# The recurrence's gate products and scans are written behind the first keys, queries and values of the forgetting attention

## The chip, the core and the metric

The kernel runs on one core of a Trainium2 chip. Its time is device time in microseconds (us), from one execution of the whole program. TensorE is written PE, VectorE DVE, ScalarE ACT, GpSimd POOL and SyncE SP. Each of them runs its own instructions strictly in the order in which they stand in its queue.

## The reference, cut to what matters

Two layers (DEPTH = 2) of a sequence encoder, 512 positions of 1024 channels, float32. Each layer mixes the positions by three branches, A, B and C, merges them with sigmoid gates, and is followed by a SwiGLU block and a gated embedding:

```
h = rmsnorm(x); z = h @ w_in            # one projection, cut into u, u_gelu, c_q, c_kv, fq, fk, fv, f_logit, gates
A: xc = causal conv of width 4 over u;  r, i = sigmoid(xc @ wa + ba), sigmoid(xc @ wx + bx)
   a = exp(-8 r softplus(-lam));  h_t = a_t h_(t-1) + sqrt(1 - a_t^2) i_t xc_t;  y_a = (h * gelu(u_gelu)) @ w_br_a
C: 8 heads: softmax(fq fk / 8 + cum_t - cum_s, causal) fv, cum = cumsum(logsigmoid(f_logit));  y_c = ... @ w_br_c
B: 8 heads of latent attention with rotary keys;  y_b = ... @ w_br_b
merged = sum over A, B, C of sigmoid(gate) * y;  x = x + merged @ w_o;  then SwiGLU and the embedding
```

The diff concerns A (the two gate products `wa`, `wx`, and the scan) and the start of C (keys and queries of heads 0 and 1, and the values of all heads).

## The kernel before

Activations lie transposed, channels on 128 partitions and the 512 positions along the row. Every float32 product is made of three matmuls of a high and a low part (`mm3`: high x high, high x low, low x high), each 128 x 128 by 512 columns. A projection of 1024 channels onto 128 (`dense`) is thus 24 matmuls into one PSUM bank, and the values of all heads (`values`) are 96 matmuls into four banks.

The weights come as one stream, in the order in which the code asks for them: SP loads units of 128 x 512 into four buffers (`raw`), and each unit is split into its two parts, the high one by a copy on ACT (L112), the low one by a subtraction on DVE (L113), into five buffers (`hl`). A unit feeds 12 matmuls, and a buffer is split anew only after PE has used it up.

Activations in split form lie in pages `pr`, plain ones in 20 pages `pf`. A page or a bank that is taken waits for its last reader. The file gives the order in which the work is written; from it a scheduler makes each engine's fixed queue when the program is built, and it may move an instruction ahead of others that would wait. It lets the splits of the weights go first.

Inside `mix(layer)`, which makes the three branches, the order is: the projections `u` with the convolution (`ev_u`: the split pages `xcp[t]` feed the gate products), the key and forget column (`key_and_forget`, whose logarithm runs on POOL), four projections for the GeLU (`ev_ug`), and then the part that the diff moves:

- the gate loop: for each of four tiles t two products of three matmuls with `xcp[t]`, and `lru_gate(t)`: on ACT two tanh out of PSUM, one exp and one tanh of the page, on DVE one instruction;
- `lru_tail`: four square roots on ACT (another function table), and for each t on DVE a fused multiply, a multiply, the scan, a fused multiply with the GeLU page, and a split into `yA[t]` (a copy on ACT, a subtraction on DVE). It then frees the pages.

After them come `fox_proj(0)` (keys `k0` and queries `q0`, 24 matmuls each, and `ev_heads`, which places them in pages for two heads and lets POOL fetch the forgetting rows), `values`, and the attention of branch C. `attention` goes through 32 blocks of 128 queries (8 heads by 4): scores S on PE, mask, maximum, exponential, normalisation on DVE and ACT, transposes on PE (L830), a split of the transposed block into `pth` (ACT, L855) and `ptl` (DVE), and, when four blocks of a head are there, the product with the values (`pv_mm`, here PV). Between the blocks it fills in matmuls of other work from a `plan`: for the first eight blocks the next heads' keys (here k1), the gates and products of branch A for two column blocks (`mg(0, 0, yA)` and `mg(0, 1, yA)`, which need all four `yA`), the reload and renormalising of x (`renorm`: eight loads on POOL, eight fused multiplies and eight subtractions on DVE, eight copies on ACT), and the next heads' queries (q1).

In the attention `self.V`, `yA` and the pages of heads 0 and 1 are what the moved part has to have made.

Of the kernel before, what the change touches and what calls it, by code (L numbers as in the profile page):

```python
# [166 lines left out]
class Trunk:  # L167
# [273 lines left out]
    def mix(self, layer):  # L441
        nc = self.nc
        L, st, X = layer, self.st, self.xp
# [6 lines left out]
        xcp = [None] * 4  # L450
# [91 lines left out]
        later = [pf.take(), pf.take()]  # L542
# [59 lines left out]
        def fox_proj(p, X, r):  # L602
            return [
                self.dense(self.win(L, C_FK + 128 * p), X, ev_heads(kp, p, r, True, False)),
                self.dense(self.win(L, C_FQ + 128 * p), X, ev_heads(qp, p, r, True, True)),
            ]

        def values(spec, X, rT):

            V = []  # L610
            bs = [self.banks.take() for _ in range(NT)]
            for k, x in enumerate(X):
                wh, wl = self.w.wide(spec + (k,))
                for j in range(NT):
                    c = slice(j * 128, (j + 1) * 128)
                    self.mm3(bs[j][:, :], x.h[:, c], x.l[:, c], wh, wl, k == 0, k == len(X) - 1)
                    yield
            for j in range(NT):
                g = pr.take()
                V.append(g)  # L620
                dst = g.ap.rearrange("p (h t d) -> p h t d", h=HEADS, t=2)
                src = bs[j].rearrange("p (h d) -> p h d", h=HEADS)
                hi = dst[:, :, 0, :]
                if rT is None:
                    self.split(hi, dst[:, :, 1, :], src)
                else:
                    r = rT[:, j:j + 1]
                    self.act(hi, src, AF.Copy, scale=r)
                    self.stt(dst[:, :, 1, :], src, r, hi.bitcast(F32), ALU.mult, ALU.subtract)
                self.banks.give(bs[j])  # L630
            self.V = V
# [6 lines left out]
        def lru_gate(t):  # L638
            def f(bR, bI):
                r, i = pf.take(), pf.take()  # L640
                self.act(r.ap, bR[:, :], AF.Tanh, bias=self.v(L, V_BA + t), scale=0.5)
                self.act(i.ap, bI[:, :], AF.Tanh, bias=self.v(L, V_BX + t), scale=0.5)
                self.banks.give(bR), self.banks.give(bI)
                s = self.sp[:, 4 * L + t:4 * L + t + 1]
                e = self.msp[:, 4 * L + t:4 * L + t + 1]
                a = pf.take()
                self.act(a.ap, r.ap, AF.Exp, bias=e, scale=e)
                last_tanh.append(self.act(r.ap, r.ap, AF.Tanh, bias=s, scale=s))
                self.stt(i.ap, i.ap, 1.0, xc[t].ap, ALU.add, ALU.mult)
                xc[t].free()  # L650
                xcp[t].free()
                aT[t], bT[t], tT[t] = a, i, r
            return f

        for t in range(4):
            bb = []
            for g in range(2):
                b = self.banks.take()
                wh, wl = self.w.tile(("lru", L, g, t))
                self.mm3(b[:, :], wh, wl, xcp[t].h, xcp[t].l, True, True)  # L660
                bb.append(b)
            lru_gate(t)(*bb)
        for p in later:
            p.free()

        def lru_tail():

            with ExitStack() as after:
                for i in last_tanh:
                    after.enter_context(self.tc.issue_after(i.ins))  # L670
                for q in tT:
                    self.act(q.ap, q.ap, AF.Sqrt, bias=self.eps[:, 1:2])
            for t in range(4):
                a, bb, q = aT[t], bT[t], tT[t]
                self.stt(q.ap, a.ap, 1.0, q.ap, ALU.add, ALU.mult)
                self.tt(bb.ap, bb.ap, q.ap)
                nc.vector.tensor_tensor_scan(q.ap, a.ap, bb.ap, 0.0, op0=ALU.mult, op1=ALU.add)  # L677
                self.stt(q.ap, q.ap, 0.25, gx[t].ap, ALU.mult, ALU.mult)
                yA[t] = pr.take()
                self.split(yA[t].h, yA[t].l, q.ap)  # L680
                for p in (q, a, bb, gx[t]):
                    p.free()

        lru_tail()
        k0, q0 = fox_proj(0, X, st["r"])
        self.run(k0)
        self.run(q0)
        self.run(values(("fv", L), X, rT))
        Xn = [None] * KD

        def renorm(*ks):
# [317 lines left out]
        for j in range(KD):  # L1009
            p = pf.take()  # L1010
# [381 lines left out]
```

## Time and profile before

| | before |
|---|---|
| median of 3 runs | 1827.87 us (1827.26 to 1827.97) |
| the profiled execution | 1827.03 us |
| its span, first to last instruction | 1825.3 us |
| mean granted TensorE clock | 0.995 |
| PE busy | 1804.1 us (99%) |
| DVE busy | 1210.6 us (66%) |
| ACT busy | 817.7 us (45%) |
| POOL busy | 117.0 us (6%) |

Busy time is the sum over the span; in a stage an engine with a low sum can still be full. In a timeline row the columns are the start, the length of the merged run (the last instruction's end, which overlaps the next start), engine, line, operation, output and inputs, count, and in brackets the idle time before it with what ended it. In a row of windows each engine has its busy time in the stretch and its count, then come the granted clock of PE, the DMA share and GB/s.

### The profile page before, as it was taken

What the parts mean: (1) busy time and instruction counts of PE and PEld (TensorE: products, weight loads), DVE (VectorE), ACT (ScalarE), POOL (GpSimd) and SP (SyncE); (2) the same over time, 40 slices, a digit from 0 to 9 for tenths busy, and PEclk for the clock granted to TensorE, in tenths of its full rate; (3) what the DMA queues carried; (4) which work ended last, traced back from release to release, by engine and by line L of the source; (5) the groups of instructions that cost most, each with busy time, mean ns of one, the idle gap of its engine ahead of it and who ended that gap; (6) DMA issues with size and microseconds to landing.
All of it is one profiled execution on the core that took longest, in us unless ns stands there. A gap on an engine that the chain in (4) does not pass through costs nothing. (4 is left out here: it accounts for less than half of the span.)

```text
span 1825.3 us, 24128 instructions
## 1 busy us (share of the span) xinstructions
PE 1804.1 (99%) x8476; PEld 1502.0 (82%) x8476; DVE 1210.6 (66%) x2421; ACT 817.7 (45%) x1562; POOL 117.0 (6%) x234
## 2 busy tenths in 40 slices
PE   9899999999999999999999999999999999999998
PEld 7678888888888888888887788888888888888887
DVE  7897678866665555444778966888576655553457
ACT  4765556553333333223447655565533333332243
POOL 1230001100000000000103200010000000000000
PEclk9899999999999999999999999999999999999999
DMA  5152223324222232322433322242242322233331
GB/s 189 59 151 82 78 80 116 96 73 139 94 98 94 97 98 98 109 94 98 132 111 122 105 81 82 89 118 85 86 129 92 99 98 96 95 110 99 98 116 47
DMA packets 98827, 184.17 MB, mean 101 GB/s; under 512 B 13553, under 2 KB 14753, under 8 KB 98705
## 3 DMA queue, kind: packets, MB, share of 16 engines
q1 hardware_dynamic: 89280, 162.04, 27.0%
q0 software_dynamic: 8416, 19.45, 3.9%
q8 instruction: 66, 1.08, 0.2%
q10 hardware_dynamic: 1008, 1.14, 0.2%
q14 instruction: 57, 0.46, 0.1%
HBM read 173.98 MB, written 4.21 MB: 98 GB/s over the span
## 5 line engine op out<-in xcount | busy, mean ns | idle before, releaser
L237 PE MATMUL bank<-pr,hl 128*128 128x512 f32 (+1 forms) x6812 | 1600.8, 392 | 7.6 <-ACT pr L233 6.9
L237 PEld LDWEIGHTS bank<-pr,hl 128*128 128x128 f32 (+1 forms) x6812 | 1268.5, 188 | 271.0 <-ACT pr L233 8.6
L112 ACT CAST hl<-raw 128x512 fp32r<-128x512 f32 x590 | 364.2, 618 | 670.3 <-PE bank L237 394.5
L113 DVE TENSOR_TENSOR hl<-raw,hl 128x512 fp32r<-128x512 f32 x590 | 404.3, 685 | 379.8 <-ACT hl L112 361.7
L221 DVE TENSOR_TENSOR pf<-pf 128x512 f32<-128x512 f32 (+3 forms) x235 | 151.1, 651 | 31.8 <-ACT pf L230 29.8
L221 DVE TENSOR_TENSOR pf<-bank,pf 128x512 f32<-128x512 f32 (+3 forms) x198 | 132.9, 676 | 57.3 <-PE bank L237 32.6
L230 ACT ACTIVATE pf<-pf 128x512 f32<-128x512 f32 (+1 forms) x145 | 86.1, 600 | 113.2 <-DVE pf L221 110.5
L237 PE MATMUL bank<-pr 128*128 128x256 f32 (+5 forms) x704 | 120.3, 302 | 3.3 <-ACT pf L230 2.5
L237 PEld LDWEIGHTS bank<-pr 128*128 128x128 f32 (+1 forms) x704 | 102.6, 190 | 13.7 <-ACT pf L230 3.3
L221 DVE TENSOR_TENSOR pr<-pf,pr 128x512 fp32r<-128x512 f32 (+3 forms) x126 | 85.5, 682 | 4.5 <-ACT pr L233 3.1
L230 ACT ACTIVATE pf<-bank,small 128x512 f32<-128x512 f32 (+3 forms) x130 | 68.9, 531 | 37.7 <-DVE small L838 34.8
L233 ACT CAST pr<-pf 128x512 fp32r<-128x512 f32 (+2 forms) x114 | 70.3, 620 | 29.5 <-DVE pf L218 20.3
L855 ACT CAST pth<-bank 128x128 fp32r<-128x128 f32 (+3 forms) x128 | 54.1, 427 | 58.5 <-PE bank L830 52.0
L221 DVE TENSOR_TENSOR ptl<-bank,pth 128x128 fp32r<-128x128 f32 (+3 forms) x128 | 61.7, 485 | 13.8 <-ACT pth L855 9.1
L838 DVE TENSOR_REDUCE small<-bank 128x1 f32<-128x128 f32 (+3 forms) x128 | 61.7, 483 | 7.6 <-PE bank L237 6.5
L237 PE MATMUL bank<-hl,pr 128*128 128x512 f32 x240 | 56.2, 390 | 0.3 <-DVE hl L113 0.3
L830 PE MATMUL bank<-identr,pf 128*128 128x128 f32 x320 | 55.0, 273 | 0.0
L237 PEld LDWEIGHTS bank<-hl,pr 128*128 128x128 f32 x240 | 44.8, 188 | 10.0 <-DVE hl L113 0.7
L225 DVE TENSOR_SCALAR pf<-pf,small 128x128 f32<-128x128 f32 (+3 forms) x128 | 48.6, 383 | 2.7
L230 ACT ACTIVATE pf<-bank,vec 128x512 f32<-128x512 f32 x60 | 41.0, 688 | 14.2 <-PE bank L237 13.8
L830 PEld LDWEIGHTS bank<-identr,pf 128*128 128x128 f32 x320 | 40.1, 140 | 8.2
L218 DVE SCALAR_TENSOR_TENSOR pf<-pf,bank 128x512 f32<-128x512 f32 x48 | 32.6, 683 | 20.8 <-PE bank L237 20.4
(112 smaller groups left out, 793.9 us busy)
## 6 DMA issues: line engine op xcount, KB each, us to landing
raw<-wst SPq DMA_DIRECT2D x606, 256.0 KB, 2.6
pf<-xT POOLq DMA_DIRECT2D x16, 256.0 KB, 3.4
pr<-pr POOLq DMA_DIRECT2D x32, 128.0 KB, 2.6
pf<-xs POOLq DMA_DIRECT2D x16, 256.0 KB, 3.3
pf<-trig POOLq DMA_DIRECT2D x12, 256.0 KB, 3.2
pf<-xT SPq DMA_DIRECT2D x8, 256.0 KB, 5.4
xs<-pf POOLq DMA_DIRECT2D x8, 256.0 KB, 2.7
pf<-pT POOLq DMA_DIRECT2D x4, 256.0 KB, 3.0
```

The costliest lines, as they stand in the source:

```text
L112: self.nc.scalar.copy(hi, src)
L113: self.nc.vector.tensor_tensor(lo, src, hi.bitcast(F32), op=ALU.subtract)
L218: self.nc.vector.scalar_tensor_tensor(out, a, s, b, op0=op0, op1=op1)
L221: self.nc.vector.tensor_tensor(out, a, b, op=op)
L225: self.nc.vector.tensor_scalar(out, a, s1, None, op0=op0)
L230: return self.nc.scalar.activation(out, a, f, **kw)
L233: self.nc.scalar.copy(hi, src)
L237: self.nc.tensor.matmul(out, a, b, start=start, stop=stop, skip_group_check=True)
L830: nc.tensor.transpose(T[:, c], p2.ap[:, c], self.ident[:, :])
L838: nc.vector.reduce_max(R[t][:, 0:1], S[:, :m], axis=AX.X, negate=True)
L855: self.nc.scalar.copy(hi, src)
```

## The change

The gate loop, with the freeing of two pages behind it, and the call of `lru_tail` move behind `k0`, `q0` and `values`. Nothing else is edited; the same instructions are issued, and the weight stream is packed in the new order.

```diff
@@ in mix(), after key_and_forget and the four GeLU projections
-        for t in range(4):
-            bb = []
-            for g in range(2):
-                b = self.banks.take()
-                wh, wl = self.w.tile(("lru", L, g, t))
-                self.mm3(b[:, :], wh, wl, xcp[t].h, xcp[t].l, True, True)
-                bb.append(b)
-            lru_gate(t)(*bb)
-        for p in later:
-            p.free()
-
         def lru_tail():
...
-        lru_tail()
         k0, q0 = fox_proj(0, X, st["r"])
         self.run(k0)
         self.run(q0)
         self.run(values(("fv", L), X, rT))
+        for t in range(4):
+            bb = []
+            for g in range(2):
+                b = self.banks.take()
+                wh, wl = self.w.tile(("lru", L, g, t))
+                self.mm3(b[:, :], wh, wl, xcp[t].h, xcp[t].l, True, True)
+                bb.append(b)
+            lru_gate(t)(*bb)
+        for p in later:
+            p.free()
+
+        lru_tail()
```

How the queues change, from the built programs. First PE in layer 0, from the last GeLU projection (bank1) on. Before (`hl` are split weights, `pr` split activations; where `hl` stands first the product is one of `values`):

```order
L237 MATMUL bank1_68<-pr_65,hl_64 128x512 x24
L237 MATMUL bank2_69<-pr_65,hl_64 128x512
L237 MATMUL bank3_70<-pr_65,hl_64 128x512
L237 MATMUL bank4_71<-pr_65,hl_64 128x512
L237 MATMUL bank7_74<-pr_65,hl_64 128x512
L237 MATMUL bank0_67<-pr_65,hl_64 128x512
L237 MATMUL bank5_72<-pr_65,hl_64 128x512
L237 MATMUL bank6_73<-pr_65,hl_64 128x512
```

The same place now:

```order
L237 MATMUL bank1_68<-pr_65,hl_64 128x512 x24
L237 MATMUL bank2_69<-pr_65,hl_64 128x512 x24
L237 MATMUL bank3_70<-pr_65,hl_64 128x512 x2
L237 MATMUL bank4_71<-hl_64,pr_65 128x512
L237 MATMUL bank7_74<-hl_64,pr_65 128x512
L237 MATMUL bank3_70<-pr_65,hl_64 128x512 x22
```

The gate products, one matmul to each of eight banks, are gone from here, and k0 (24 matmuls into bank2) and q0 (bank3) follow the GeLU projections at once.

The second place is PE in layer 0 where the first transposes of the attention stand (L830), before:

```order
L237 MATMUL bank3_70<-pr_65,hl_64 128x512 x14
L237 MATMUL bank0_67<-pr_65 128x256 x2
L237 MATMUL bank3_70<-pr_65,hl_64 128x512 x8
L237 MATMUL bank5_72<-pr_65,hl_64 128x512 x18
L830 MATMUL bank7_74<-identr_77,pf_66 128x128
L237 MATMUL bank5_72<-pr_65,hl_64 128x512 x5
L830 MATMUL bank2_69<-identr_77,pf_66 128x128 x2
L237 MATMUL bank5_72<-pr_65,hl_64 128x512
L830 MATMUL bank4_71<-identr_77,pf_66 128x128 x3
L830 MATMUL bank6_73<-identr_77,pf_66 128x128 x4
```

Now (bank5 x24 is the gate of `mg(0, 1)`; bank0 and bank7 are the products of branch A with `yA`):

```order
L237 MATMUL bank5_72<-pr_65,hl_64 128x512 x24
L237 MATMUL bank1_68<-pr_65 128x128 x2
L237 MATMUL bank6_73<-pr_65 128x512 x2
L830 MATMUL bank7_74<-identr_77,pf_66 128x128
L237 MATMUL bank0_67<-pr_65,hl_64 128x512
L830 MATMUL bank2_69<-identr_77,pf_66 128x128 x2
L830 MATMUL bank4_71<-identr_77,pf_66 128x128 x3
L237 MATMUL bank0_67<-pr_65,hl_64 128x512 x3
L237 MATMUL bank7_74<-pr_65,hl_64 128x512 x4
L237 MATMUL bank0_67<-pr_65,hl_64 128x512 x3
```

Fewer matmuls stand ahead of the transposes, and the products with `yA` are cut into threes and fours among them.

The third place is DVE in layer 0. Before, while PE makes the values, DVE runs the recurrence (L677 is the scan; `pf<-pf` with L218 and L221 its multiplies):

```order
L218 SCALAR_TENSOR_TENSOR pf_66<-pf_66 128x512 x2
L221 TENSOR_TENSOR pf_66<-pf_66 128x512
L218 SCALAR_TENSOR_TENSOR pf_66<-pf_66 128x512
L221 TENSOR_TENSOR pf_66<-pf_66 128x512
L221 TENSOR_TENSOR pr_65<-pf_66,pr_65 8x512
L677 SCALAR_TENSOR_TENSOR pf_66<-pf_66 128x512
L113 TENSOR_TENSOR hl_64<-raw_63,hl_64 128x512
```

Now the same multiplies and the scan (its line is L666 there) stand behind the eviction of k1 and the first masks and maxima of the softmax:

```order
L838 TENSOR_REDUCE small_85<-bank4_71 128x1
L218 SCALAR_TENSOR_TENSOR pf_66<-pf_66 128x512 x2
L221 TENSOR_TENSOR pf_66<-pf_66 128x512
L218 SCALAR_TENSOR_TENSOR pf_66<-pf_66 128x512
L221 TENSOR_TENSOR pf_66<-pf_66 128x512
L113 TENSOR_TENSOR hl_64<-raw_63,hl_64 128x512
L666 SCALAR_TENSOR_TENSOR pf_66<-pf_66 128x512
L844 RECIPROCAL small_85<-small_85 128x1
```

All four scans have moved from the stage of the values into that of the first head's softmax. Layer 1 is changed in the same way; ACT loads a function table ten times in the program instead of eight, since in layer 0 the square roots now stand between the softmax exponentials.

## The prediction

> **What bounds the kernel now.** I read the page's busy shares first:
>
> ```profile
> PE 1804.1 (99%) x8476; PEld 1502.0 (82%) x8476; DVE 1210.6 (66%) x2421; ACT 817.7 (45%) x1562; POOL 117.0 (6%) x234
> PE   9899999999999999999999999999999999999998
> DVE  7897678866665555444778966888576655553457
> ```
>
> PE is the bound, and its idle 21 us (1825.3 less 1804.1) lie mostly at two places, the starts of the two layers, which are also where DVE is nearly full (slices 1 to 8 and 20 to 23). So the question is what PE waits for there. PE's timeline in layer 0, from the GeLU projections to the first PV, then the granted clock in windows:
>
> ```profile
> 40.89 13.76 PE L237 MATMUL bank<-pr,hl 128*128 128x512 f32 x60
> 58.45 0.75 PE L237 MATMUL bank<-pr,hl 128*128 128x512 f32 x2 [3.81 <-ACT pr L233]
> 60.42 1.22 PE L237 MATMUL bank<-pr,hl 128*128 128x512 f32 x2 [1.22 <-ACT pr L233]
> 63.49 18.39 PE L237 MATMUL bank<-pr,hl 128*128 128x512 f32 x68 [1.85 <-ACT pr L233]
> 81.72 21.92 PE L237 MATMUL bank<-hl,pr 128*128 128x512 f32 x96
> 103.48 0.33 PE L237 MATMUL bank<-pr 128*128 128x128 f32 x2
> ...
> 143.22 0.22 PE L237 MATMUL bank<-ptl,pr 128*64 128x128 f32 x1
> ```
>
> ```profile
> 60.00:68.00 8.00, 5.73 (x13) 4.01 (x14) 8.00 (x15) 4.91 (x9) 0.00 (x0) 0.50 0.14 45
> 68.00:70.00 2.00, 2.00 (x8) 1.59 (x7) 1.54 (x5) 2.00 (x5) 0.18 (x1) 0.68 0.00 0
> 70.00:72.00 2.00, 2.00 (x11) 1.65 (x10) 1.61 (x3) 2.00 (x5) 1.66 (x5) 1.00 0.00 0
> ```
>
> At 54.65 (40.89 + 13.76) the gate products begin. They wait for ACT's copies of the convolved tiles (L233), and those for DVE, busy for all of 60 to 68. During the wait the clock falls to 0.50, and it stays there until about 69.3 (0.68 of full over 68 to 70), 5.8 us after PE has work again. PV of head 0 ends at 143.44.
>
> In layer 1 the same stretch:
>
> ```profile
> 935.93 40.56 PE L237 MATMUL bank<-pr,hl 128*128 128x512 f32 x178
> 976.33 16.71 PE L237 MATMUL bank<-hl,pr 128*128 128x512 f32 x73
> ...
> 1012.53 5.76 PE L237 MATMUL bank<-pr,hl 128*128 128x512 f32 x24 [0.64 <-DVE hl L113]
> 1018.13 0.33 PE L237 MATMUL bank<-pr 128*128 128x128 f32 x2
> ...
> 1023.08 0.74 PE L237 MATMUL bank<-pr 128*128 128x512 f32 x2 [2.24 <-ACT pf L230]
> 1041.43 0.22 PE L237 MATMUL bank<-ptl,pr 128*64 128x128 f32 x1
> ```
>
> The 178 matmuls to 976.33 run at 0.227 us each without a wait, the gate products among them: here the convolution is done in time. The small waits come later, and the 2.24 us before 1023.08 do not lower the clock.
>
> Both stretches do the same PE work: counted in the queue, the matmuls from the gates' start to the end of PV equal 331 of 512 columns. The 96 of the values take 21.76 us (81.72 to 103.48), 0.227 each, the 24 from 1012.53 to 1018.13 0.233, so I take 0.23: 76.1 us. Layer 0 needs 143.44 - 54.65 = 88.8, so it loses 12.7 us. Layer 1 begins the part at 976.33 - 72 x 0.227 = 960.0 and ends at 1041.65: 81.7, a loss of 5.5. That sum, 18.2 us, is all that a better order could win here.
>
> **What the move takes away.** In layer 0 k0 follows the GeLU projections at once. Its weights are split (four units are ahead), its input was ready long before, and its bank was evicted early; q0 and the values likewise. When the gates come, some 33 us later, the convolved tiles (PE's last wait for them ended at 63.49 before) are long there. So the 6.9 us of waiting and the slow clock go: I count the whole 12.7 as gained, and the 5.5 of layer 1 too, and charge every new wait below.
>
> **What the move adds.** It displaces DVE's and ACT's work. DVE before, in windows:
>
> ```profile
> 960.00:1000.00 40.00, 39.69 (x176) 32.52 (x175) 33.11 (x55) 30.64 (x51) 13.62 (x28) 1.00 0.33 106
> 1000.00:1040.00 40.00, 36.53 (x168) 29.21 (x167) 39.31 (x83) 29.19 (x61) 10.10 (x20) 1.00 0.40 127
> 60.00:80.00 20.00, 15.11 (x29) 0.77 0.19 57
> 100.00:120.00 20.00, 19.94 (x33) 1.00 0.45 137
> ```
>
> (the third number of the first two rows is DVE's, the second of the last two.) DVE has 6.9 us of slack while the keys, queries and values run (33.11 of 40) and none while the attention begins (39.31 of 40). The recurrence now leaves the stretch with slack and enters the full one. Whether PE feels it is decided by one stretch of queues: from the end of k1 (bank1 x24, behind the gates) to PV of head 0. DVE evicts k1 first, and must then go through everything that stands ahead of the last `ptl` split before PV can go on. I count its instructions in the new queue and price them by the spacing of starts in these rows (the second number is the duration, which overlaps the next):
>
> ```profile
> 998.60 1.21 DVE L677 TENSOR_TENSOR_SCAN pf<-pf 128x512 f32<-128x512 f32 x1
> 999.73 0.66 DVE L221 TENSOR_TENSOR pr<-pf,pr 128x512 fp32r<-128x512 f32 x1
> ...
> 1015.93 0.67 DVE L221 TENSOR_TENSOR pf<-bank,pf 128x512 f32<-128x512 f32 x1
> 1016.53 0.67 DVE L113 TENSOR_TENSOR hl<-raw,hl 128x512 fp32r<-128x512 f32 x1
> 1017.13 0.73 DVE L218 SCALAR_TENSOR_TENSOR pf<-pf,vec 128x512 f32<-128x512 f32 x1
> 1017.79 0.68 DVE L221 TENSOR_TENSOR pr<-pf,pr 128x512 fp32r<-128x512 f32 x1
> ...
> 1030.58 0.68 DVE L838 TENSOR_REDUCE small<-bank 128x1 f32<-128x512 f32 x1
> 1031.18 0.34 DVE L225 TENSOR_SCALAR pf<-pf,small 128x256 f32<-128x256 f32 x1
> 1031.44 0.29 DVE L221 TENSOR_TENSOR bank<-bank,fmask 128x128 f32<-128x128 f32 x1
> 1031.64 0.41 DVE L225 TENSOR_SCALAR pf<-pf,small 128x384 f32<-128x384 f32 x1
> ```
>
> A full row costs 0.60, with a vector operand 0.66, a scan 1.13 to 1.15, the masks, maxima and normalisations 0.20 to 0.60 by width.
>
> Layer 0: 40 full rows, 7 of them with a vector (24.6), 4 scans (4.6), 26 small (6.8): 36.0 us. Layer 1: 37 full rows (22.8), 4 scans (4.6), 21 small (5.7): 33.0 us. Of these the recurrence is 12 multiplies, 4 scans and 4 low parts, 14.3 us; most of the renormalising comes here too, since the pages it needs are freed by the recurrence.
>
> PE's own work in the same stretch, to the end of PV, is only 100 matmuls (23.0 us) in layer 0 and 87 (20.0) in layer 1; after the last `ptl` split some 0.9 us of it is left. PE thus waits at least 36.0 + 0.9 - 23.0 = 13.9 us, and 33.0 + 0.9 - 20.0 = 13.9: together 27.8, where before it lost 18.2. The wait will be spread over the first transposes, which need the normalised blocks, and the products with `yA`. No fill hides it: matmuls behind PV stand behind it in PE's queue.
>
> Three more terms. First, DVE's waits for ACT within the stretch. ACT's prices:
>
> ```profile
> 67.18 0.82 ACT L230 ACTIVATE pf<-pf,msp 128x512 f32<-128x512 f32 x1
> 67.91 1.25 ACT L230 ACTIVATE pf<-bank,vec 128x512 f32<-128x512 f32 x2
> ...
> 80.14 2.42 ACT L566 CAST pr<-pf 64x512 fp32r<-64x512 f32 x4 [0.55 <-DVE pf L221]
> 83.42 1.28 ACT L230 ACT_TABLE_LOAD   x1
> 84.71 1.95 ACT L230 ACTIVATE pf<-pf,eps 128x512 f32<-128x512 f32 x3
> ...
> 124.23 0.37 ACT L230 ACTIVATE pf<-bank,small 128x128 f32<-128x128 f32 x1
> 126.24 0.47 ACT L230 ACTIVATE pf<-bank,small 128x256 f32<-128x256 f32 x1
> ```
>
> In layer 0, from k1's eviction to the second softmax exponential, ACT has the last exp and two tanh of the gates (0.7 each), four weight copies (0.5 to 0.6), four head copies (2.4), four square roots (2.5), four table loads (5.1) and two exponentials (0.8): some 15 us. DVE's work up to the reciprocal of that block is 12.5, so it is held 2.5 us or a little more. In layer 1, up to the first multiply by a square root, ACT has 6.6 us and DVE 3.7: 2.9. I take 5.7 in all (bounds 0, if DVE starts late, and 12, twice that). The two added table loads are inside. Second, DVE's full stretches run about 2% over the sum of spacings: 1.4 on 69. Third, the clock. Walked through with these prices, the queues have PE waiting 3 to 5 us at a time before the first transposes; 3.81 us halved the clock and 2.24 did not. Where it halves, the loss inside the wait is free, and the 5.8 us at half rate after it cost 2.9. For two layers that is 0 to 5.8; I take 2.9.
>
> The Trainium skill, "TensorE: Matmul & The Clock Gate", Part 1, says that the gate halves the clock after an idle window of about 3.4 us and opens after a busy one as long. The drop agrees with the 3.81 us here; the return took 5.8, and by the page's 3.4 a layer would pay an estimated 1.7 us instead of 2.9, so the sum would be about 1 lower.
>
> What costs nothing: the forgetting chain (POOL's logarithm, DVE's cumulative scan, POOL's fetches to the head pages) slips behind weight splits, but by the same walk it lands some 4 us ahead of the score matmul that needs it; without that cover it would cost what it is late. POOL's eight renormalising loads move behind the head fetches and wait for freed pages; the stream asks for their rows only late in the stretch. SP's stream is as long as before. The gates' banks are those of the GeLU, q0 and the values; the last four are free as soon as the values are evicted, which the queue has put first.
>
> Sum: 27.8 + 5.7 + 1.4 + 2.9 - 18.2 = 19.6 us. On the profiled execution's 1827.03 that is 1846.6; the median of the runs is 0.8 above it, so 1847.
>
> **The rivals.**
>
> Faster: what decides is DVE's stretch against PE's. If the attention absorbed the recurrence as it absorbs the renormalising before (DVE full from 1000 to 1040 and PE losing only about 5 us), the layer-0 stall would go and the new waits stay near the 5.5 of layer 1 before in all: 1827 - 12.7 = 1814 to 1815. For it speaks the slack of PE's fill; against it that it holds only where the waits come below 9.1 us a layer, that is DVE's stretch below some 30 us where I count 36 and 33. Chance 0.07.
>
> No change: the layers cancel, with waits about as large as the 18.2 gained; needs 9 to 10 us less than I count, for instance no ACT wait and no slow clock, and a PE that runs 0.22 a matmul after the stall. 1827 to 1829. Chance 0.07.
>
> Much slower: the clock halves at the first wait and does not come back before PV, because PE is never busy long enough. Then the 23.0 and 20.0 us of PE work take 46.0 and 40.0 and are longer than DVE's 36.9 + 2.8 and 33.9 + 2.9: 6.3 + 3.2 more, and 2.9 more for the second layer's return: 1847 + 12.4, about 1859. For it speaks that the products come in threes and fours between waits; against it that while DVE holds PE, PE's half rate is hidden. Chance 0.13.
>
> **How the numbers follow.** The main case, slower by 11 to 27 us with the clock low for part of the time, gets 0.73 and its sum is the forecast, 1847. The low end is the floor alone: 27.8 - 18.2 = 9.6 without any further wait, 1837; I go to 1836. The high end takes in the slow clock: 1860. Left out are the faster and unchanged cases, 0.14. A difference of 0.2% (3.7 us) is about what a measurement of this kernel can tell from none. Faster 0.07, same 0.06, slower 0.87 (the rest of the second rival falls just above).
>
> **What would show it.** Right: in layer 0 no wait of PE between the GeLU projections and the attention, clock 1.00 there, and S of the first block some 10 us earlier than the 103.48 of before; then waits of PE of about 14 us or more per layer between the end of k1 and PV of head 0, put down to DVE's normalisations and to the low parts of `yA`; DVE full there and idle while the values run; two more table loads in layer 0. PV of head 0 near 139 in layer 0, and in layer 1 as late as before though 50 fewer matmuls stand ahead of it. Wrong: if PE streams through k1 and the products with `yA` without waits, or if the values' stage stalls instead, because DVE or ACT, waiting in order for PE's buffers, hold up an eviction.

## The result, and the profile after

The changed kernel takes 1846.62 us (median of 4 runs, 1845.5 to 1847.65) against 1827.61 for the kernel before: a ratio of 1.0104, 95% interval 1.0091 to 1.0117, or 19.0 us more. The forecast was 1847. The profiled execution took 1846.69 us with a span of 1844.9, 19.6 more than the span before.

The page after, busy shares and slices:

```profile
PE 1811.6 (98%) x8476; PEld 1506.6 (82%) x8476; DVE 1213.8 (66%) x2421; ACT 821.2 (45%) x1564; POOL 115.2 (6%) x234
PE   9979999999999999999999799999999999999998
DVE  7887678866665555444876976788666655553456
```

The dent in PE's row has moved from slice 2 (the gates of layer 0) to slice 3, and a second one stands in slice 23, in layer 1. DVE's work is the same (1213.8 against 1210.6 us), but in layer 1 its row now falls to 6 in slice 22, just ahead of the dent, where it had 8; in layer 0 the slices are too coarse to show it. PE's waits over the whole run, in total, times and the longest:

```profile
PE bank L830 <- DVE pf L225: 9.6, 4, 5.6
PE bank L237 <- ACT pr L233: 8.8, 5, 3.5
PE bank L237 <- DVE pr L221: 4.8, 3, 2.4
```

PE's timeline in layer 0, then in layer 1:

```profile
41.80 19.66 PE L237 MATMUL bank<-pr,hl 128*128 128x512 f32 x86
...
92.80 0.22 PE L237 MATMUL bank<-pr 128*128 128x128 f32 x1
...
110.68 0.86 PE L237 MATMUL bank<-pr 128*128 128x128 f32 x4
117.11 0.47 PE L830 MATMUL bank<-identr,pf 128*128 128x128 f32 x1 [5.57 <-DVE pf L225]
117.50 0.79 PE L237 MATMUL bank<-pr,hl 128*128 128x512 f32 x1
120.73 0.69 PE L830 MATMUL bank<-identr,pf 128*128 128x128 f32 x2 [2.44 <-DVE pf L225]
...
134.66 0.66 PE L830 MATMUL bank<-identr,pf 128*128 128x128 f32 x4 [1.14 <-DVE pf L225]
135.93 1.91 PE L237 MATMUL bank<-pr,hl 128*128 128x512 f32 x4 [0.60 <-DVE pr L221]
...
142.51 0.22 PE L237 MATMUL bank<-ptl,pr 128*64 128x128 f32 x1
```

```profile
943.96 35.12 PE L237 MATMUL bank<-pr,hl 128*128 128x512 f32 x154
...
1028.01 1.22 PE L237 MATMUL bank<-pr,hl 128*128 128x512 f32 x2 [3.51 <-ACT pr L233]
1032.26 2.93 PE L237 MATMUL bank<-pr,hl 128*128 128x512 f32 x6 [2.39 <-DVE pr L221]
1040.19 0.84 PE L237 MATMUL bank<-pr,hl 128*128 128x512 f32 x2 [2.72 <-ACT pr L233]
1043.52 4.16 PE L237 MATMUL bank<-pr,hl 128*128 128x512 f32 x8 [1.26 <-ACT pr L233]
...
1049.54 0.22 PE L237 MATMUL bank<-ptl,pr 128*64 128x128 f32 x1
```

From 41.80 to 110.68 PE never waits; the stall at the gates is gone and S of the first block comes at 92.80 (103.48 before). Then it waits eight times in layer 0 (13.3 us) and four times in layer 1 (9.9 us). PV of head 0 ends at 142.73, nearly where it ended before, though 38 fewer matmuls stand ahead of it.

For every run below I use three points of the trace: the start of the matmuls behind the last `onesr` product in layer 0 (40.89 before, 41.80 now), the same in layer 1 (935.93 and 943.96), and the end of the span. The stretch between the first two is what layer 0 costs, the one after them layer 1. So the 19.6 us are 0.9 (a later start; the traces of all the runs, the first 40 us written alike, have that point anywhere between 40.8 and 42.2, so it is no part of the change), 7.1 in layer 0 and 11.6 in layer 1.

### The profile page after: what moved, and what is told of

The parts are those of the page before. It is cut to its first block, busy times and chain, and to the rows that moved or that the text cites. A ratio compares the mean times of both kernels' runs of the same rounds, so it can differ in the third digit from the quotient of the medians.

```text
span 1844.9 us, 24103 instructions
## 1 busy us (share of the span) xinstructions
PE 1811.6 (98%) x8476; PEld 1506.6 (82%) x8476; DVE 1213.8 (66%) x2421; ACT 821.2 (45%) x1564; POOL 115.2 (6%) x234
## 4 chain that ended last, share of the span: by engine, by line
PE 94%; DVE 3%; ACT 2%; issue 1%; DMA 0%; DVEq 0%; ACTq 0%
PE bank L237 93%; PE bank L830 2%; DVE pf L218 1%; ACT pf L230 1%; DVE pr L221 0%; DVE pf L666 0%; ACT L230 0%; DVE pf L221 0%; ACT hl L112 0%; DVE hl L113 0%; DVE pf L225 0%; ACT pr L566 0%; DVE ptl L221 0%; DVE small L838 0%; DMA pf<-pf 0%
## 5 line engine op out<-in xcount | busy, mean ns | idle before, releaser
L237 PEld LDWEIGHTS bank<-pr,hl 128*128 128x128 f32 (+1 forms) x6812 | 1270.7, 188 | 278.6 <-ACT pr L233 11.1
L221 DVE TENSOR_TENSOR pf<-pf 128x512 f32<-128x512 f32 (+3 forms) x235 | 151.2, 652 | 31.9 <-ACT pf L230 29.9
L221 DVE TENSOR_TENSOR pf<-bank,pf 128x512 f32<-128x512 f32 (+3 forms) x198 | 132.9, 676 | 56.8 <-PE bank L237 32.8
L237 PE MATMUL bank<-pr 128*128 128x256 f32 (+4 forms) x704 | 120.9, 302 | 0.0
L221 DVE TENSOR_TENSOR pr<-pf,pr 128x512 fp32r<-128x512 f32 (+3 forms) x126 | 85.3, 682 | 5.2 <-ACT pr L233 4.0
L230 ACT ACTIVATE pf<-bank,small 128x128 f32<-128x128 f32 (+3 forms) x130 | 68.9, 531 | 32.7 <-DVE small L838 29.8
L233 ACT CAST pr<-pf 128x512 fp32r<-128x512 f32 (+2 forms) x114 | 70.3, 620 | 23.9 <-DVE pf L218 14.6
L221 DVE TENSOR_TENSOR ptl<-bank,pth 128x128 fp32r<-128x128 f32 (+3 forms) x128 | 61.7, 484 | 11.8 <-ACT pth L855 8.0
L830 PE MATMUL bank<-identr,pf 128*128 128x128 f32 x320 | 57.8, 280 | 9.7 <-DVE pf L225 9.6
L830 PEld LDWEIGHTS bank<-identr,pf 128*128 128x128 f32 x320 | 40.9, 143 | 20.2 <-DVE pf L225 12.0
L218 DVE SCALAR_TENSOR_TENSOR pf<-pf,bank 128x512 f32<-128x512 f32 x48 | 32.4, 683 | 20.8 <-PE bank L237 20.3
```

The source lines that it names most:

```text
L218: self.nc.vector.scalar_tensor_tensor(out, a, s, b, op0=op0, op1=op1)
L221: self.nc.vector.tensor_tensor(out, a, b, op=op)
L230: return self.nc.scalar.activation(out, a, f, **kw)
L233: self.nc.scalar.copy(hi, src)
L237: self.nc.tensor.matmul(out, a, b, start=start, stop=stop, skip_group_check=True)
L830: nc.tensor.transpose(T[:, c], p2.ap[:, c], self.ident[:, :])
```

## The experiments

Twelve kernels were run, each beside the kernel before. "L0" and "L1" are what its trace adds to the two stretches of before; they hold one profiled execution each and are good to a microsecond or two (runs 7 and 11 write layer 0 alike and read -7.8 and -5.9).

| run | order in layer 0 / layer 1 | median us | ratio to before (95%) | L0 | L1 |
|---|---|---|---|---|---|
| changed kernel | k q V G T / same | 1846.6 | 1.0104 (1.0091 to 1.0117) | +7.1 | +11.6 |
| 1 | k q V G T / G T k q V | 1834.9 | 1.0033 (1.0021 to 1.0045) | +7.1 | +0.2 |
| 2 | G T k q V / k q V G T | 1839.7 | 1.0058 (1.0045 to 1.0071) | -0.2 | +12.6 |
| 3 | k q G T V / same | 1830.3 | 1.0012 (1.0003 to 1.0021) | +0.4 | +2.3 |
| 4 | k q G T V / G T k q V | 1829.2 | 1.0006 (0.9997 to 1.0014) | +1.1 | +0.1 |
| 5 | changed kernel, late renorm | 1831.8 | 1.0019 (1.0010 to 1.0028) | -2.2 | +7.3 |
| 6 | before, late renorm | 1822.5 | 0.9969 (0.9958 to 0.9981) | -2.7 | -2.6 |
| 7 | k q G T V / same, late renorm | 1814.1 | 0.9924 (0.9910 to 0.9937) | -7.8 | -5.0 |
| 8 | changed kernel without scans | 1835.5 | 1.0039 (1.0025 to 1.0052) | +2.2 | +5.7 |
| 9 | G k q V T / same | 1830.3 | 1.0010 (1.0001 to 1.0019) | +2.4 | +0.8 |
| 10 | changed kernel without square roots | 1844.5 | 1.0086 (1.0073 to 1.0100) | +5.2 | +12.5 |
| 11 | k q G T V / G T k q V, late renorm | 1817.9 | 0.9940 (0.9927 to 0.9954) | -5.9 | -2.4 |
| 12 | G k q V T, T's DVE part tied behind V | 1850.3 | 1.0120 (1.0103 to 1.0137) | +12.5 | +9.9 |

(G the gate loop, T `lru_tail`, k and q the first keys and queries, V the values; before is G T k q V.)

**Runs 1 and 2: one layer at a time.** The gate loop became a function `lru_gates()`, and the order depends on `L`:

```diff
+        if L == 0:                       # run 2: if L == 1
+            self.run(k0); self.run(q0); self.run(values(...)); lru_gates(); lru_tail()
+        else:
+            lru_gates(); lru_tail(); self.run(k0); self.run(q0); self.run(values(...))
```

> The move is made in layer 0 alone; layer 1 has the old order. Theory (each layer pays for DVE's stretch between the end of k1 and PV of head 0, less what its old stall gave back): by the two traces layer 0 costs 7.1 us and the later start 0.9, so 7 to 8 us slower than before, 1835. PV of head 0 in layer 0 near 142 us, in layer 1 a loss of about 5.5 us as before. Rival (the layers are coupled: layer 0's late pages or the shifted weight stream make part of layer 1's loss): well over 8 us slower. Rival (the removed stall of 12.7 us outweighs the new waits in layer 0, all of the loss is layer 1's): not slower than before.

> The move is made in layer 1 alone; layer 0 has the old order. Theory: the whole loss is paid by layer 1's own stretch, about 11.7 us, so 1839 to 1840, and with the layer 0 run the two differences add up to the 19 us of the whole change. Rival (coupled layers): the sum of the two differences misses 19 us by more than 3.

Measured: 7.4 and 12.1 us over the before of the same call; together 19.5, the whole change 19.0. As far as these runs can tell the layers do not touch each other, and layer 0 loses in spite of the 12.7 us of stall that it gave back.

**Runs 3 and 4: the recurrence between q0 and the values.** The same functions in the order k0, q0, `lru_gates()`, `lru_tail()`, values; in run 4 in layer 0 alone.

> In both layers the gates and the recurrence stand behind k0 and q0 but ahead of the values. Theory (the loss comes from the recurrence entering DVE's full stretch behind k1, not from delaying it as such): 48 matmuls, 11 us, stand ahead of the gates, more than the 6.9 us that PE waited for the convolved tiles, and the recurrence still runs under the values; layer 0's loss of 12.7 us goes and no wait of 14 us comes, layer 1 stays near its 5.5. So 8 to 12 us faster than before, 1816 to 1820. Rival (any delay of the recurrence is paid at the transposes, since DVE has no slack behind it): layer 0 gains its 12.7 and pays back 10 or more of them, 1825 to 1835.

> As the run with the recurrence between q0 and the values, but in layer 0 alone; layer 1 has the old order. Theory: the gain is layer 0's alone (its stall was the only one to remove), so 8 to 12 us faster than before, and equal to the run with both layers or up to 3 us better, because layer 1 had no stall at its gates. Rival (layer 1 also gains): this run 3 us or more slower than the one with both layers.

My theory missed by some 10 us and the rival was right. In run 3 the stall at the gates (6.9 us) is gone, and PE pays as much again: 1.54 us of waiting at 106.89 and 7.0 in the rows below.

```profile
116.66 0.49 PE L237 MATMUL bank<-pr,hl 128*128 128x512 f32 x1 [3.04 <-ACT pr L233]
119.72 0.80 PE L237 MATMUL bank<-pr,hl 128*128 128x512 f32 x1 [2.57 <-ACT pr L233]
...
123.20 10.80 PE L237 MATMUL bank<-pr,hl 128*128 128x512 f32 x37 [1.38 <-DVE pr L221]
...
143.55 0.22 PE L237 MATMUL bank<-ptl,pr 128*64 128x128 f32 x1
```

PV of head 0 ends at 143.77. It ended at 143.44 before and at 142.73 in the changed kernel: three orders of PE's work, one time to within about a microsecond. So it does not look as if PE's order sets it.

**Runs 5 to 7: ten microseconds of DVE's work taken out.** If PV comes when DVE has gone through its queue, then work that need not be there should be worth its length. `renorm` (16 rows of DVE per layer, some 10 us) moves into the plan of the next eight blocks; the projections until then take x unnormalised, as the earlier ones do:

```diff
-            [fp(1, 0, X, st["r"]), (renorm(0, 1), 0), mg(0, 0, yA, X, st["r"]), (renorm(2, 3, 4), 0),
-             mg(0, 1, yA, X, st["r"]), (renorm(5, 6, 7), 0), (drop_x(), 0), fp(1, 1), mg(0, 2, yA)],
-            [fp(2, 0), mg(0, 3, yA), mg(0, 4, yA), fp(2, 1), mg(0, 5, yA)],
+            [fp(1, 0, X, st["r"]), mg(0, 0, yA, X, st["r"]), mg(0, 1, yA, X, st["r"]),
+             fp(1, 1, X, st["r"]), mg(0, 2, yA, X, st["r"])],
+            [fp(2, 0, X, st["r"]), (renorm(0, 1), 0), mg(0, 3, yA, X, st["r"]), (renorm(2, 3, 4), 0),
+             mg(0, 4, yA, X, st["r"]), (renorm(5, 6, 7), 0), (drop_x(), 0), fp(2, 1), mg(0, 5, yA)],
```

> The changed kernel, with the renormalising of x (8 fused multiplies and 8 subtractions on DVE, some 10 us per layer) moved from the plan of the first eight blocks into that of the second; the projections between take x unnormalised and scale at their eviction. Theory (DVE's backlog ahead of PV of head 0 sets the wait, and any 10 us of DVE's work taken out of it are worth 10 us of PE): about 20 us less than the changed kernel's 1846.6, 1823 to 1832, that is level with before. Rival (the wait is for what the recurrence itself feeds, the normalised blocks behind it and yA, through ACT's queue and its table loads, not for DVE's sum): 1842 to 1847.

> The order of before, with the renormalising moved into the second plan as in the run above. Theory: layer 0's 12.7 us at the gates are untouched by it up to the values, but PE's small waits of layer 1's attention (5.5 us) go, and in layer 0 nothing waited in the attention before; 1821 to 1825. Rival (DVE's backlog behaves as a sum over the whole stretch, and the order before also runs at DVE's pace to PV): no more than that either, since PE has no further wait to lose there. If the renormalising only moves the crowding into the second plan: 1827 or more.

> The recurrence between q0 and the values in both layers, and the renormalising in the second plan. Theory: the run with the recurrence there alone had no stall at the gates but waits of 8.5 us and a slow clock behind k1, because DVE's backlog, 44 us without a gap, was merely moved; with 10 us of it taken out those waits go: 10 to 14 us below the 1830.3 of that run, 1815 to 1820, faster than before by 8 or more. Rival (the waits hang on the recurrence's own chain): 1826 to 1831.

The changed kernel gets 14.8 us back by it (1846.6 to 1831.8): 9.3 in layer 0, as expected, but only 4.3 in layer 1. Run 6 has the same late renormalising without the move; beside it the move costs 0.5 us in layer 0 and still 9.9 in layer 1. There 5.0 us of PE's waits stay ahead of PV of head 0 (2.87, 0.17, 1.06, 0.32 and 0.59), and the second plan, where the renormalising now stands, has 2.0 us of waits and 3.4 us of half clock. So this run bears out the theory for layer 0; in layer 1 it moved part of the crowding, and how much of the 11.6 us there is the length of DVE's queue and how much the late recurrence itself is left open by it. The order of run 3 gets 16.2 back and is then 14 us faster than before (1814.1 against 1828.5), the fastest of all. Before itself gains 6.0, as much as forecast, but 2.7 of it in layer 0, where the theory had none to gain. In run 7 these are PE's waits, but for those ahead of the first products and one of 0.2 us:

```profile
PE bank L237 <- ACT pf L230: 1.9, 1, 1.9
PE bank L237 <- DVE hl L113: 1.3, 2, 1.0
```

Compare runs 6 and 7 in layer 0: -2.7 with the stall at the gates, -7.8 without it. The stall that I had priced at 12.7 us is worth about 5 once DVE's backlog no longer takes its place, and nothing (runs 3 and 4) while it does.

**Run 8: DVE's scans left out.** The scan is dropped and the multiply behind it reads its input, so the recurrence along the positions is not computed; PE's and ACT's work stays.

```diff
-                nc.vector.tensor_tensor_scan(q.ap, a.ap, bb.ap, 0.0, op0=ALU.mult, op1=ALU.add)
-                self.stt(q.ap, q.ap, 0.25, gx[t].ap, ALU.mult, ALU.mult)
+                self.stt(q.ap, bb.ap, 0.25, gx[t].ap, ALU.mult, ALU.mult)
```

> The changed kernel without the four scans per layer (the multiply that follows reads the scan's input), which takes 4.6 us per layer from DVE's queue ahead of PV of head 0 and nothing from ACT or PE. Theory (DVE's queue is what PE waits for): 4.6 us less in each layer, 1846.6 - 9.2 = 1837, bounds 1835 to 1840. Rival (ACT's queue or the table loads set the wait): 1844 to 1847.

11.1 us less than the changed kernel, 4.9 and 5.9 by layer: DVE's 4.6 a layer and a little more; the mean clock is 0.992 where the changed kernel had 0.990. A scan is a part of DVE's queue and of the recurrence's own chain, so by itself this run excludes ACT but does not tell those two apart; run 5, in layer 0, does.

**Run 10: ACT's table loads.** The square roots become copies with the same bias (so the roots are not computed), and ACT loads 4 tables in the program instead of 10.

```diff
-                    self.act(q.ap, q.ap, AF.Sqrt, bias=self.eps[:, 1:2])
+                    self.act(q.ap, q.ap, AF.Identity, bias=self.eps[:, 1:2])
```

> The changed kernel with the four square roots per layer replaced by a plain copy with the same bias, so that ACT loads no other function table (in layer 0 three table loads of 1.28 us fewer between the first softmax exponentials); ACT's copies themselves stay. Theory (DVE waited for ACT only 2.9 us in the layer-0 stretch and 0.2 in that of layer 1): 1 to 4 us less than the changed kernel, 1843 to 1846. Rival (ACT's table loads, 5.1 us in layer 0, hold up the exponentials that the first transposes need): 6 us less or more, 1841 and below.

2.1 us between the medians, with intervals that overlap; the traces put it in layer 0 (+5.2 for +7.1). ACT's tables are a small part at most: the rival's 1841 and below was not reached by any run (the lowest is 1843.4).

**Runs 9 and 12: the tail alone.** Run 9 leaves `lru_gates()` in its old place and calls `lru_tail()` behind the values.

> The gate products stay where they were before, ahead of k0 in both layers; only the recurrence's tail (square roots, multiplies, scans, splits) stands behind the values. Theory A (DVE's pace sets PV of head 0, and PE's waits ahead of it are one sum, wherever they fall): layer 0's wait of 6.9 us at the gates is there again, but PE then waits about as much less behind k1, and the time is within 4 us of the changed kernel's, 1843 to 1850. Theory B (the ledger of the prediction: each wait of PE is a loss of its own, so the stall kept is added to the new waits): 12.7 us over the changed kernel, 1856 to 1860.

1830.3 lies outside both ranges, and the run tested neither theory. The scheduler put DVE's scans back where their inputs were ready: the first at 89.29 and the last at 101.29, in the order before at 89.33 and 101.32. The 1.7 us that it costs were not followed up. Run 12 ties DVE's rows of the tail behind the last eviction of the values (the low part of V[3]):

```diff
+                    self.v_low = nc.vector.scalar_tensor_tensor(...)   # in values(), the same instruction
...
             for t in range(4):
+                behind = self.tc.issue_after(self.v_low.ins)
+                behind.__enter__()
                 a, bb, q = aT[t], bT[t], tT[t]
```

> As the run with the tail alone behind the values, where the scheduler pulled the scans forward again to where they stood before; here DVE's part of the tail (multiplies, scans, low parts) is tied in its queue behind the last eviction of the values. The gates, ACT's square roots and the order of the weights stay where that run has them. Theory A (what hurts is DVE's recurrence leaving the stage of the values, where DVE has slack, for the stretch to PV, where it has none): the whole loss of the change comes back without moving a gate product, and since layer 0's wait at the gates is kept too, at least the changed kernel's time, 1844 to 1858; PV of head 0 in layer 0 later than 143 us. Theory B (what hurts is the move of the gates: ACT's tanh and exp behind the values' copies): as the run with the tail alone, 1828 to 1833.

Theory A holds: 1850.3, without a gate product moved. DVE in the stage of the values and behind it, before, in the changed kernel and in run 12 (its busy time is the third number):

```profile
84.00:104.00 20.00, 20.00 (x91) 16.61 (x90) 19.43 (x29) 13.29 (x22) 6.16 (x12) 1.00 0.44 134
104.00:144.00 40.00, 39.39 (x184) 31.87 (x183) 38.66 (x84) 27.58 (x57) 9.20 (x19) 1.00 0.40 120
```

```profile
84.00:104.00 20.00, 20.00 (x92) 16.66 (x91) 13.55 (x24) 18.33 (x30) 5.40 (x13) 1.00 0.26 85
104.00:144.00 40.00, 26.74 (x101) 19.02 (x100) 38.01 (x75) 26.50 (x48) 12.31 (x24) 0.83 0.32 96
```

```profile
84.00:104.00 20.00, 20.00 (x91) 16.60 (x90) 10.94 (x18) 13.99 (x23) 3.06 (x6) 1.00 0.35 114
104.00:144.00 40.00, 32.18 (x124) 23.92 (x123) 39.91 (x78) 21.82 (x43) 14.15 (x28) 0.86 0.36 117
```

DVE is full from 104 to 144 in all three. What differs is how long it sat idle before: 0.6, 6.5 and 9.1 of 20 us. (In layer 1 likewise: DVE is busy for 17.05 of 20 us from 980 on before, 11.17 from 988 on in the changed kernel and 12.97 from 995 on in run 12.) An engine that is full to the end of a stretch cannot make up for such time. The sizes do not match one for one: in the 20 us ahead of these, DVE is busy for 14.07, 16.29 and 14.68 us, so from 64 to 104 it idles 3.7 and 7.9 us more than before, where layer 0 costs 7.1 and 12.5. PE's busy time behind 104 falls in both, but not in that order, since in run 12 PE also has its stall at the gates behind it and so more work left. In run 12, where the stall at the gates is kept as well, layer 0 costs 12.5, 5.4 more than in the changed kernel.

**Run 11: layer 1's order with the late renormalising.**

> As the run at 1814 (recurrence between q0 and the values, renormalising in the second plan), but with the recurrence of layer 1 at its old place ahead of k0. Layer 1 had no wait at its gates to remove; with the late renormalising and the old order it waited 2 us in all, with the new order not at all. Theory: the order of layer 1 is worth what it waited, 2 to 5 us, so 1816 to 1819. Rival (what the order is worth lies in layer 0 alone): 1813 to 1815.

1817.9, as the theory had it: the new order is worth 2.6 us (by the traces) to 3.8 (by the medians) in layer 1 too, where it cost 2.3 without the late renormalising (run 3). The sign of such a move depends on whether DVE has room behind it.

## Why the prediction was right, and where it was not

The total was right within a microsecond, and its cause (DVE's recurrence leaves a stretch with slack for one without) is shown by run 12, in which DVE's rows alone are held back, with run 8, and with run 5 in layer 0; run 5 leaves open what part of layer 1's loss is the sum of DVE's queue. By its steps:

**The stall goes.** Right as a fact: no wait up to 110.68, S of the first block 10.7 us earlier. As a price it holds only beside the charge for new waits; runs 3, 6 and 7 put its own worth at 0 to 5 us, not 12.7.

**The floor, 36.0 and 33.0 us of DVE.** From k1's eviction to the last `ptl` split, layer 0:

```profile
99.39 0.69 DVE L221 TENSOR_TENSOR pf<-bank,pf 128x512 f32<-128x512 f32 x1 [0.66 <-PE bank L237]
...
101.87 0.69 DVE L113 TENSOR_TENSOR hl<-raw,hl 128x512 fp32r<-128x512 f32 x1 [1.19 <-ACT hl L112]
...
107.06 1.31 DVE L218 SCALAR_TENSOR_TENSOR pf<-pf 128x512 f32<-128x512 f32 x2 [1.34 <-ACT pf L230]
...
138.26 0.68 DVE L221 TENSOR_TENSOR ptl<-bank,pth 128x512 fp32r<-128x512 f32 x1
```

138.26 + 0.60 - 99.39 = 39.5 us, where the sum (36.0, 2.8 for ACT, 0.7 of gaps) was 39.5. Layer 1 took 34.9 (1012.28 to 1046.58 + 0.60) where it was 36.6.

**DVE's waits for ACT, 5.7.** Mis-sized by about half: 2.9 in layer 0 (the rows above and one of 0.34), but 0.2 in layer 1, where I had 2.9.

**The clock and the end of PV, 4.7** (2.9, and 0.9 a layer). PV ended 3.9 us (142.73 less 138.86) and 2.6 us (1049.76 less 1047.18) behind the last split: 6.5. In layer 0 the clock was at half there until 139.56 (below); in layer 1 it was full from 1047.50 on, and more of PE's work was left than the 0.9 counted.

**The layers.** They were forecast at 6.2 and 13.4, and cost 7.1 and 11.6; with the 0.9 of the later start, which is no part of the change, the errors cancel. So the hit within a microsecond is partly luck, that within two or three is not.

**The traces' signs.** "PV of head 0 near 139" was wrong: its own terms, the clock and the gaps included, give 141, and it came at 142.7. "Waits of about 14 us or more per layer" showed as 13.3 and 9.9, because the rest of the loss is mostly slow matmuls and not idle time: by the count of the prediction (from 55.56 and 968.03, as far behind the starts of the two stretches as before, and with 293 and 280.5 matmuls of 512 columns now, 38 and 50.5 fewer) layer 0 loses 142.73 - 55.56 - 293 x 0.23 = 19.8 and layer 1 1049.76 - 968.03 - 280.5 x 0.23 = 17.2; of these 37.0 us the waits are 23.1, and 13.9 are not. In the four spells of half clock (last section) PE was busy for 21.6 us, so 10.8 of the 13.9 are matmuls at half rate. The sum's 2.9 for the clock cannot be set against them: it counted only the half rate behind the wait and took the rest as hidden while DVE holds PE. One sign held closely: in layer 1 PV ends 105.8 us behind the start of its stretch, against 105.7 before, with 50.5 fewer matmuls ahead of it. The two table loads more came too (10 against 8). And in layer 1 the profile names ACT's high parts of `yA` (L233) more than DVE's rows. ACT was a small part at most: mostly its copies waited for DVE's multiply.

```profile
1026.82 0.62 ACT L112 CAST hl<-raw 128x512 fp32r<-128x512 f32 x1 [1.29 <-DMA raw<-wst]
1027.35 0.61 ACT L233 CAST pr<-pf 128x512 fp32r<-128x512 f32 x1
1029.64 0.62 ACT L233 CAST pr<-pf 128x512 fp32r<-128x512 f32 x1 [1.68 <-DVE pf L218]
...
1032.90 0.62 ACT L233 CAST pr<-pf 128x512 fp32r<-128x512 f32 x1 [1.14 <-DVE pf L218]
...
1037.19 1.28 ACT L233 CAST pr<-pf 128x512 fp32r<-128x512 f32 x2 [0.83 <-DVE pf L218]
...
1039.52 0.62 ACT L233 CAST pr<-pf 128x512 fp32r<-128x512 f32 x1 [0.45 <-DVE pf L218]
...
1042.84 0.62 ACT L233 CAST pr<-pf 128x512 fp32r<-128x512 f32 x1
```

The copies that end PE's waits at 1028.01, 1040.19 and 1043.52 are those that start at 1027.35, 1039.52 and 1042.84. The second waited for DVE. The third began when DVE's multiply (1042.07, 0.74 long) was through. The first began some 0.7 us after its multiply, behind a weight copy whose load had come late: that much of the 3.51 us is not DVE's.

**The rivals.** "Faster" asked for a DVE stretch below some 30 us. With 10 us of DVE's work out, the order of the change does not reach it (run 5, 1831.8). Run 7 lands at the 1814 that it named, but in another order and with 7.8 us from layer 0 and 5.0 from layer 1, where the rival had 12.7 from layer 0 alone: the number agrees by chance. "No change" was added up wrongly: it needs 19.6 us less than the sum, 9.6 less than the floor alone, while the missing ACT wait and slow clock that it names take off 8.6 and leave some 1838. The half clock of "much slower" came, but went again after 3.4 to 10.2 us each time.

**Smaller readings.** Of PE's 21 us idle before, 11.3 lie at the two layers' starts (46 to 145 and 930 to 1042); 8.9 are in the last 25 us of the program, which the prediction passes over. The clock did not fall during the wait of 3.81 us but 0.6 us after it (59.04; PE had work at 58.45). And 40 full rows at the prediction's own prices are 24.4 us, not 24.6. None of this moves the forecast.

## What to carry to other kernels

When an engine that feeds the bottleneck is full up to the end of a stretch, ask what a move makes it do in the time before: what it idles there it cannot win back later, wherever the bottleneck's own waits are then seen. Here, removing a visible stall gained nothing while such a backlog stood behind it (runs 3 and 4), and about 5 us once the backlog was shortened (run 7). And a call that is written later is not run later if the scheduler finds its inputs ready (run 9): look at the queue before reading a result.

## What the hardware showed that was not expected

The granted clock does not follow the length of a single wait. I had argued from two rows (3.81 us halved it, 2.24 did not). In run 9 a wait of 1.99 us, ahead of 125.88, was followed by half clock, and one of 3.02 us, ahead of 1026.39, was not (the clock is the third number from the end of a row):

```profile
123.00:126.00 3.00, 1.01 (x7) 0.75 (x6) 2.97 (x6) 2.93 (x6) 1.64 (x4) 1.00 0.52 169
126.00:128.00 2.00, 2.00 (x8) 1.64 (x9) 1.91 (x5) 1.98 (x4) 1.32 (x3) 0.84 0.47 132
128.00:130.00 2.00, 2.00 (x7) 1.52 (x6) 2.00 (x6) 1.79 (x6) 1.12 (x3) 0.50 0.31 71
...
1023.00:1026.00 3.00, 0.37 (x3) 0.19 (x2) 3.00 (x7) 2.94 (x5) 0.76 (x2) 1.00 0.26 83
1026.00:1028.00 2.00, 1.61 (x7) 1.35 (x8) 1.94 (x4) 1.92 (x6) 0.81 (x2) 1.00 0.53 143
```

And in the changed kernel it fell at 136, when PE was busy again, after 8 us of short waits (none above 1.8) in which PE was busy for 3.39:

```profile
128.00:136.00 8.00, 3.39 (x13) 1.76 (x13) 8.00 (x17) 4.59 (x10) 0.00 (x0) 1.00 0.02 10
136.00:139.00 3.00, 3.00 (x8) 2.31 (x9) 3.00 (x7) 2.27 (x5) 0.54 (x1) 0.52 0.33 90
```

Read in windows of 1 us (a share between 0.50 and 1.00 tells where in it the clock changed), the spells of half clock last 10.24 us before (59.04 to 69.28), 10.24 and 3.42 in layer 0 of the changed kernel (115.66 to 125.90, 136.14 to 139.56), 10.24 and 6.84 in its layer 1 (1027.02 to 1037.26, 1040.66 to 1047.50), 10.24 in run 3 and 3.40 in run 9: one, two or three times 3.41 us (run 8 has one of four, 114.19 to 127.84), never anything between. Their starts and ends fit one grid: from 115.66 to 1027.02 in the changed kernel are 267 times 3.4133 us. The clock is thus decided once in 3.41 us, at times of its own, and a wait that lies across such a time may count for less than a shorter one that does not. The Trainium skill, "TensorE: Matmul & The Clock Gate", Part 1, gives a free-running window of 3413 ns; the spells agree with it to 0.02 us. Its wording of an idle window does not cover the last two fences, in which PE was never idle that long. The traces show what comes nearer. Cut at the grid, PE was busy for at most 0.50 of the 3.41 us just ended ahead of 32 of the 33 falls of the clock in the two layers of all fourteen traces (0.54 ahead of the other, in run 8), and for at least 0.50 in every one behind which the clock stayed full. In run 9 the wait of 3.02 us is cut by a border at 1025.08 (0.50 and 0.62 on its two sides), and the one of 1.99 lies whole in one stretch (0.44). In the last microseconds of the programs the clock fell behind shares of up to 0.69, so the busy share is not the whole rule. The prediction's return of 5.8 us was no constant but what was left, after PE had work again, of a spell of three such periods; in the changed kernel the same spell left 3.4 (steady work from 122.45).
